# A hybrid decoder trunk on one core: high and low parts of transposed blocks split bank by bank

## The chip, the core and the metric
The kernel runs on one NeuronCore of a Trainium2 chip. Times are microseconds (us) of device time of one execution. TensorE (PE, with its weight loads as PEld) does the matmuls and transposes, VectorE (DVE) and ScalarE (ACT) read its results out of PSUM, GpSimd (POOL) does small arithmetic, and SyncE (SP) issues nearly all DMAs. PSUM has eight banks of 512 fp32 values per partition; this kernel keeps five for accumulators (`acc`) and three for transposes and small products (`pst`).

## What is computed
Two layers of a decoder on x of 256 x 1024 in fp32. Every sub-layer is normed before and after and added to x:

```python
for l in range(DEPTH):
    x = x + 0.5 * rmsnorm(swiglu(rmsnorm(x, ffn1_pre_g[l]), w_ffn1_in[l], w_ffn1_out[l]), ffn1_post_g[l])
    h = rmsnorm(x, mix_pre_g[l])
    (z, xbc, dt_raw, rq, rk, rv, rg, aq, ak, av, gate) = jnp.split(h @ w_in[l], offsets, axis=-1)
    ...
    branch = jnp.einsum('blmc,mcd->blmd', ys, w_branch[l])
    y = jnp.sum(gates * branch, axis=2) @ w_out[l]
    x = x + rmsnorm(y, mix_post_g[l])
    x = x + 0.5 * rmsnorm(swiglu(rmsnorm(x, ffn2_pre_g[l]), w_ffn2_in[l], w_ffn2_out[l]), ffn2_post_g[l])
```

`ys` stacks three mixers (a state-space one, retention, windowed attention). Inner width of the FFN is 2816.

## The kernel before, in words
The rows of x are two tiles of 128 tokens, t = 0 and 1. There are six phases: FFN 1, mixer, FFN 2 of layer 0, then the same of layer 1. Precision is kept by splitting every operand of a large matmul into a high part (rounded to fp32r) and a low part (what the rounding left), and by three matmuls for each block of 128 input channels (`mm3`, lines 86 to 89: high x low and high x high at line 88, low x high at line 89). ScalarE makes the high part with a copy, VectorE the low part with a subtraction that reads the source again (`split`, lines 66 to 69). Weights come in by DMA as `raw`, are split into `hl` (a ring of eight tiles, two blocks of channels each) and are used from there.

Activations must have channels on partitions, so they are transposed on TensorE, four blocks of 128 x 128 to a PSUM bank, and split on the way out. That happens in three places. `prenorm` (lines 169 to 190) transposes x of one t in two banks of four blocks; ScalarE writes each block's high part times the gain (line 182), VectorE its low part (line 185); the two squares of the row scale (line 150, in `sumsq`) are queued on ScalarE behind the last high part, and GpSimd turns their sums into the scale (lines 141 and 143). `transposed` (lines 153 to 164) does the same for the SwiGLU product `h` (two blocks to a bank, `hT`), for the mixers' outputs (`yT`, eight blocks) and their gated sum (`ysT`, four blocks), two blocks to one split. `att_kv` (lines 357 to 380) reads keys and values out of the accumulator: high parts `kh`, low parts `kl`, value `vn`, and multiplies them by a reversing matrix on TensorE (lines 375 and 379).

A phase begins inside the phase before it. `close` (line 308) runs its last four gemms and, within the last, calls the next prenorm for t = 0, whose transposes stand at a fixed place among the matmuls (lines 104 to 111). The next phase's first gemm uses that xT, unscaled: the row scale r is applied to the gemm's result. In the FFN the first result goes through silu (`sl`, line 125) and a product (`h`, line 127) to the transposes at line 161; the prenorm of t = 1 is called at the third step of the gemm of the second column chunk (lines 327 and 336). In the mixer the first result is that of `kvdt` (line 756): dt on VectorE (`dtx`, line 758), then `att_kv`; the prenorm of t = 1 is called in the middle of `aq0` (line 789). That prenorm needs x of t = 1, which `postnorm` (line 206) updates after the square and the product of lines 196 and 197.

The program order is a wish only. A scheduler with its own timeline puts the instructions of each engine in a fixed order, earlier program lines first among those that it holds to be ready. It also keeps two engines from using one PSUM bank at the same time, reads included, by waits in that order.

Of the kernel before, what the change touches and what calls it, by code (L numbers as in the profile page):

```python
# [8 lines left out]
F32 = mybir.dt.float32  # L9
R = mybir.dt.float32r  # L10
AF = mybir.ActivationFunctionType
ALU = mybir.AluOpType
AX = mybir.AxisListType

P = 128
# [25 lines left out]
class Trunk:  # L41
# [111 lines left out]
    def transposed(self, dst, src, t):  # L153
        nc = self.nc
        ts = slice(t * P, t * P + P)
        n = src.shape[-1] // P
        for q in range(0, n, 4):
            m = min(4, n - q)
            ps = self.pst.tile([P, 4, P], F32, tag="pst", name="pT")
            for j in range(m):  # L160
                nc.tensor.transpose(ps[:, j], src[:, (q + j) * P:(q + j + 1) * P], self.ident)  # L161
            for j in range(0, m, 2):
                d = dst[(q + j) // 2]
                self.split(d[:, :, 0, ts], d[:, :, 1, ts], ps[:, j:j + 2])

    def new_T(self, n, name):
        return [self.t4([2, 2, T], R, name) for _ in range(n)]
# [1 line left out]
    def prenorm(self, xT, t, g, r):  # L169

        nc = self.nc
        x = self.x
        ts = slice(t * P, t * P + P)
        made = []
        for q in range(0, KD, 4):
            ps = self.pst.tile([P, 4, P], F32, tag="pst", name="pT")
            for j in range(4):
                made.append(nc.tensor.transpose(ps[:, j], x[:, t, (q + j) * P:(q + j + 1) * P], self.ident))  # L178
            for j in range(4):
                k = q + j  # L180
                hi, lo = xT[k // 2][:, k % 2, 0, ts], xT[k // 2][:, k % 2, 1, ts]
                last = nc.scalar.activation(out=hi, in_=ps[:, j], func=AF.Copy, scale=g[:, k:k + 1])  # L182
                if k == 1:
                    self.opened = last
                nc.vector.scalar_tensor_tensor(out=lo, in0=ps[:, j], scalar=g[:, k:k + 1], in1=hi.bitcast(F32),  # L185
                                               op0=ALU.mult, op1=ALU.subtract)
        with self.tc.issue_after(last.ins):
            ss = self.sumsq([x[:, t, 0:512], x[:, t, 512:1024]], 1.0 / 32)
        self.rstd(ss, EPS, r)
        return made  # L190
# [166 lines left out]
    def att_kv(self, t, ps):  # L357
        nc, S = self.nc, self.S
        if t == 0:
            S["kT"] = self.t4([2, 2, T], R, "kT")  # L360
            S["av"] = self.t1([NT, P], name="av")
        k3 = ps[:, 0:P].rearrange("p (g d) -> p g d", g=2)
        kh = self.t1([2, 2, 64], R, name="kh")
        kl = self.t1([2, 2, 64], R, name="kl")
        r = S["r"][t]
        for o in range(2):
            nc.scalar.activation(out=kh[:, :, o], in_=k3, func=AF.Copy, scale=r)
            nc.vector.scalar_tensor_tensor(out=kl[:, :, o], in0=k3, scalar=r, in1=kh[:, :, o].bitcast(F32),
                                           op0=ALU.mult, op1=ALU.subtract)
        vn = self.t1([P], name="vn")  # L370
        nc.scalar.activation(out=vn, in_=ps[:, P:2 * P], func=AF.Copy, scale=r)
        pT = self.pbank()
        for g in range(2):
            for i, k in enumerate((kh, kl)):
                nc.tensor.matmul(pT[:, 2 * g + i], k[:, g].rearrange("p o d -> p (o d)"), self.revr,
                                 start=True, stop=True)
        self.copy(S["kT"][:, :, :, P - t * P:T - t * P], pT.rearrange("p (g o) n -> p g o n", g=2))
        pv = self.pbank()
        nc.tensor.matmul(pv[:, 0], self.revr.bitcast(F32), vn, start=True, stop=True)
        self.copy(S["av"][:, 1 - t], pv[:, 0])  # L380
# [587 lines left out]
```

## Time and profile before
| | |
|---|---|
| median of 3 runs | 1517.14 us (1514.94 to 1518.55) |
| the profiled execution | 1515.11 us |
| its span, first to last instruction | 1513.3 us |
| mean granted TensorE clock | 0.991 |
| instructions | 19964 |
| TensorE matmuls, waits of TensorE listed in the trace | 7277; 7 kinds, 18.3 us |

The profile shows one execution. Busy time is the share of the span in which an engine worked; for every idle stretch the trace names what ended it. The granted clock is that of TensorE, 1.00 being 2.4 GHz. Matmuls overlap, so the distance of their starts, not their length, is the pace.

### The profile page before, as it was taken

The page shows a single profiled execution, that of the slowest core. Times are in us where ns is not written, and L with a number is a line of the kernel's source. Part 1 is how long each engine was busy: PE and PEld are TensorE (multiplying, and loading weights), DVE is VectorE, ACT ScalarE, POOL GpSimd, SP SyncE. Part 2 cuts the span into 40 slices and gives each one's busy share as a digit, 9 for nine tenths or more (in the row PEclk, how much of TensorE's full clock was granted, in tenths as well). Part 3 has the DMA queues.
Part 4 walks back from the last instruction along what each step waited for, and adds up shares of the span by engine and source line. Part 5 has one row for each costly group of instructions (what it writes and reads, how often), then busy time and mean ns, then how long its engine had stood idle before and what let it go on. Part 6 is the DMA issues. An engine that isn't in the chain of part 4 may idle for free.

```text
span 1513.3 us, 19964 instructions
## 1 busy us (share of the span) xinstructions
PE 1488.2 (98%) x7277; PEld 1236.5 (82%) x7277; DVE 998.5 (66%) x1647; ACT 808.3 (53%) x1392; POOL 40.4 (3%) x80
## 2 busy tenths in 40 slices
PE   8999999999999999999999999999999999999998
PEld 6788878888888887888878888788888888778886
DVE  6654566778887676555566554767798876765643
ACT  6454465576554466444465454656665544655541
POOL 0000010000100000000000000000000000000000
PEclk9999999999999999999999999999999999999999
DMA  8654546545565555554555545564455655644551
GB/s 309 225 177 167 165 162 232 167 144 162 184 223 181 195 172 180 197 188 163 186 193 187 200 151 167 201 196 155 153 167 181 208 177 176 218 166 168 192 173 67
DMA packets 82771, 275.28 MB, mean 182 GB/s; under 512 B 11120, under 2 KB 15856, under 8 KB 82672
## 3 DMA queue, kind: packets, MB, share of 16 engines
q1 hardware_dynamic: 82384, 273.93, 53.9%
q8 instruction: 57, 0.93, 0.3%
q14 instruction: 42, 0.34, 0.1%
q10 hardware_dynamic: 288, 0.07, 0.0%
HBM read 272.86 MB, written 1.11 MB: 181 GB/s over the span
## 4 chain that ended last, share of the span: by engine, by line
PE 61%; issue 36%; DVE 1%; ACT 1%; POOL 1%; DMA 0%; SPq 0%; POOLq 0%; DVEq 0%; ACTq 0%
PE acc L88 32%; PE acc L89 16%; PE xbc L88 3%; PE xbc L89 2%; PE pT L161 1%; PE pS L420 1%; PE py L697 1%; PE po L455 1%; PE pT L178 1%; PE pb L447 1%; PE po L528 0%; DMA raw<-w_ffn_in 0%; DVE xT L185 0%; ACT xT L182 0%; ACT junk L150 0%
## 5 line engine op out<-in xcount | busy, mean ns | idle before, releaser
L88 PE MATMUL acc<-hl,xT 128*128 128x512 f32 (+1 forms) x2496 | 776.2, 393 | 3.1 <-DVE hl L69 3.0
L69 DVE TENSOR_TENSOR hl<-raw,hl 128x1024 fp32r<-128x1024 f32 (+2 forms) x544 | 592.2, 1105 | 183.0 <-ACT hl L68 164.0
L68 ACT CAST hl<-raw 128x1024 fp32r<-128x1024 f32 (+2 forms) x544 | 512.1, 956 | 255.4 <-PE acc L89 216.7
L88 PEld LDWEIGHTS acc<-hl,xT 128*128 128x128 f32 x2496 | 463.9, 189 | 95.6 <-DVE hl L69 3.2
L89 PE MATMUL acc<-hl,xT 128*128 128x512 f32 (+1 forms) x1248 | 486.7, 393 | 0.4 <-DVE xT L185 0.4
L89 PEld LDWEIGHTS acc<-hl,xT 128*128 128x128 f32 x1248 | 235.4, 189 | 49.0 <-DVE xT L185 1.4
L88 PE MATMUL acc<-hl,hT 128*128 128x512 f32 x704 | 216.9, 390 | 0.0
L88 PEld LDWEIGHTS acc<-hl,hT 128*128 128x128 f32 x704 | 131.7, 188 | 26.9
L89 PE MATMUL acc<-hl,hT 128*128 128x512 f32 x352 | 136.4, 389 | 0.0
L88 PE MATMUL acc<-hl,yT 128*128 128x512 f32 x384 | 122.1, 398 | 0.0
L127 DVE SCALAR_TENSOR_TENSOR h<-acc,pr,sl 128x256 f32<-128x256 f32 x88 | 42.2, 480 | 119.6 <-ACT sl L125 119.5
L125 ACT ACTIVATE sl<-acc,pr 128x256 f32<-128x256 f32 x88 | 41.9, 476 | 145.2 <-PE acc L89 144.8
L88 PEld LDWEIGHTS acc<-hl,yT 128*128 128x128 f32 x384 | 71.5, 188 | 16.7 <-issue 2.4
L89 PEld LDWEIGHTS acc<-hl,hT 128*128 128x128 f32 x352 | 66.1, 188 | 13.9
L89 PE MATMUL acc<-hl,yT 128*128 128x512 f32 x192 | 75.5, 393 | 0.0
L88 PE MATMUL xbc<-xT,hl 128*128 128x256 f32 x384 | 72.0, 286 | 0.0
L88 PEld LDWEIGHTS xbc<-xT,hl 128*128 128x128 f32 x384 | 60.2, 191 | 2.1 <-issue 1.5
L68 ACT CAST hT<-pT 128x256 fp32r<-128x256 f32 x88 | 32.6, 372 | 44.9 <-PE pT L161 44.8
L89 PE MATMUL xbc<-xT,hl 128*128 128x256 f32 x192 | 55.4, 289 | 0.0
L69 DVE TENSOR_TENSOR hT<-pT,hT 128x256 fp32r<-128x256 f32 x88 | 36.9, 420 | 26.9 <-ACT hT L68 26.9
L197 DVE TENSOR_TENSOR yg<-acc,gain 128x512 f32<-128x512 f32 x24 | 16.6, 690 | 46.9 <-ACT junk L196 46.9
L182 ACT ACTIVATE xT<-pT,pg 128x128 fp32r<-128x128 f32 x96 | 32.0, 364 | 21.7 <-DVE xT L185 13.9
(189 smaller groups left out, 1166.4 us busy)
## 6 DMA issues: line engine op xcount, KB each, us to landing
raw<-w_ffn_in SPq DMA_DIRECT2D x176, 512.0 KB, 4.8
raw<-w_main SPq DMA_DIRECT2D x152, 512.0 KB, 4.4
raw<-w_ffn_out SPq DMA_DIRECT2D x88, 512.0 KB, 4.7
raw<-w_branch SPq DMA_DIRECT2D x48, 512.0 KB, 4.4
raw<-w_out SPq DMA_DIRECT2D x16, 512.0 KB, 4.0
bias<-rows SPq DMA_DIRECT2D x8, 512.0 KB, 6.3
L<-acs SPq DMA_DIRECT2D x8, 512.0 KB, 6.2
gain<-b_gate SPq DMA_DIRECT2D x6, 512.0 KB, 5.1
```

The source lines that it names most:

```text
L68: nc.scalar.copy(out=hi, in_=src)
L69: nc.vector.tensor_tensor(out=lo, in0=src, in1=hi.bitcast(F32), op=ALU.subtract)
L88: return (mm(ps, xh, wl, start=start, stop=False), mm(ps, xh, wh, start=False, stop=False), mm(ps, xl, wh, start=False, stop=stop))
L89: mm(ps, xl, wh, start=False, stop=stop))
L125: self.last_silu = nc.scalar.activation(out=sl, in_=a, func=AF.Silu, scale=r)
L127: nc.vector.scalar_tensor_tensor(out=h, in0=b, scalar=r, in1=sl, op0=ALU.mult, op1=ALU.mult)
L161: nc.tensor.transpose(ps[:, j], src[:, (q + j) * P:(q + j + 1) * P], self.ident)
L178: made.append(nc.tensor.transpose(ps[:, j], x[:, t, (q + j) * P:(q + j + 1) * P], self.ident))
L182: last = nc.scalar.activation(out=hi, in_=ps[:, j], func=AF.Copy, scale=g[:, k:k + 1])
L197: self.nc.vector.tensor_tensor(out=y, in0=ps, in1=g[:, 512 * i:512 * i + 512], op=ALU.mult)
L420: nc.tensor.matmul(pS[:, i, :w], qT[t][:, hb + j + i], kT[:, g, hl, ks], start=hl == 0, stop=hl == 1)
L447: nc.tensor.transpose(pp[:, j], s[:, j, b * P:b * P + P], self.ident)
```

## The change
The number of instructions and their shapes stay. In `prenorm` all four high parts of a bank are issued before its four low parts. In `transposed` all high parts of a bank (one or two instructions) come before its low parts. In `att_kv` both high parts and the value come before both low parts.

```diff
@@ transposed
-            for j in range(0, m, 2):
-                d = dst[(q + j) // 2]
-                self.split(d[:, :, 0, ts], d[:, :, 1, ts], ps[:, j:j + 2])
+            parts = [(dst[(q + j) // 2], ps[:, j:j + 2]) for j in range(0, m, 2)]
+            for d, p in parts:
+                nc.scalar.copy(out=d[:, :, 0, ts], in_=p)
+            for d, p in parts:
+                nc.vector.tensor_tensor(out=d[:, :, 1, ts], in0=p, in1=d[:, :, 0, ts].bitcast(F32), op=ALU.subtract)
@@ prenorm
-            for j in range(4):
-                k = q + j
-                hi, lo = xT[k // 2][:, k % 2, 0, ts], xT[k // 2][:, k % 2, 1, ts]
+            part = lambda k, o: xT[k // 2][:, k % 2, o, ts]
+            for k in range(q, q + 4):
+                hi, j = part(k, 0), k - q
                 last = nc.scalar.activation(out=hi, in_=ps[:, j], func=AF.Copy, scale=g[:, k:k + 1])
                 if k == 1:
                     self.opened = last
-                nc.vector.scalar_tensor_tensor(out=lo, in0=ps[:, j], scalar=g[:, k:k + 1], in1=hi.bitcast(F32),
-                                               op0=ALU.mult, op1=ALU.subtract)
+            for k in range(q, q + 4):
+                nc.vector.scalar_tensor_tensor(out=part(k, 1), in0=ps[:, k - q], scalar=g[:, k:k + 1],
+                                               in1=part(k, 0).bitcast(F32), op0=ALU.mult, op1=ALU.subtract)
@@ att_kv
         for o in range(2):
             nc.scalar.activation(out=kh[:, :, o], in_=k3, func=AF.Copy, scale=r)
+        vn = self.t1([P], name="vn")
+        nc.scalar.activation(out=vn, in_=ps[:, P:2 * P], func=AF.Copy, scale=r)
+        for o in range(2):
             nc.vector.scalar_tensor_tensor(out=kl[:, :, o], in0=k3, scalar=r, in1=kh[:, :, o].bitcast(F32),
                                            op0=ALU.mult, op1=ALU.subtract)
-        vn = self.t1([P], name="vn")
-        nc.scalar.activation(out=vn, in_=ps[:, P:2 * P], func=AF.Copy, scale=r)
```

## Rows read from the trace of the kernel before
**Rows 1.** The page, part 1: busy time of each engine, share, instructions.
```profile
PE 1488.2 (98%) x7277; PEld 1236.5 (82%) x7277; DVE 998.5 (66%) x1647; ACT 808.3 (53%) x1392; POOL 40.4 (3%) x80
```
**Rows 2.** Waits of TensorE: waiting engine and line, for what: us, times, longest.
```profile
PE pT L161 <- DVE h L127: 6.4, 3, 2.4
PE pb L375 <- ACT kh L367: 4.9, 2, 2.5
PE acc L88 <- DVE hl L69: 3.0, 1, 3.0
PE pb L375 <- DVE kl L368: 1.7, 2, 0.9
```
**Rows 3.** Waits of all engines, ScalarE's for the low part in prenorm.
```profile
ACT xT L182 <- DVE xT L185: 13.9, 35, 0.8
```
**Rows 4.** Timeline, mixer of layer 0: start, busy us, engine, line [idle before, releaser].
```profile
197.44 0.36 ACT L182 ACTIVATE xT<-pT,pg 128x128 fp32r<-128x128 f32 x1
...
198.74 1.05 ACT L68 CAST hl<-raw 128x1024 fp32r<-128x1024 f32 x1 [0.94 <-PE acc L89]
...
202.75 0.63 ACT L182 ACTIVATE xT<-pT,pg 128x128 fp32r<-128x128 f32 x2 [0.78 <-DVE xT L185]
...
203.15 0.61 DVE L185 SCALAR_TENSOR_TENSOR xT<-pT,pg,xT 128x128 fp32r<-128x128 f32 x2 [0.18 <-ACT xT L182]
...
203.80 0.37 ACT L182 ACTIVATE xT<-pT,pg 128x128 fp32r<-128x128 f32 x1 [0.42 <-DVE xT L185]
...
204.59 0.37 ACT L182 ACTIVATE xT<-pT,pg 128x128 fp32r<-128x128 f32 x1 [0.42 <-DVE xT L185]
...
206.80 0.56 POOL L143 TENSOR_TENSOR pr<-v,mhalf 128x1 f32<-128x1 f32 x1
```
**Rows 5.** Timeline of TensorE, same stretch: before the wait, and back at full pace.
```profile
206.40 0.29 PE L89 MATMUL acc<-hl,xT 128*128 128x272 f32 x1
...
214.11 0.62 PE L88 MATMUL acc<-hl,xT 128*128 128x512 f32 x2
```
**Rows 6.** Chain that ended last, in order of time: start, us, what, how many.
```profile
22.97 1.36 PE acc L88 x6
...
562.03 0.87 PE pT L178 x8
```
**Rows 7.** Busy time by stretch: PE, PEld, DVE, ACT, POOL, granted clock, DMA share, GB/s.
```profile
211.00:212.00 1.00, 1.00 (x7) 1.00 (x7) 0.20 (x1) 0.58 (x1) 0.00 (x0) 0.50 0.01 4
```
**Rows 8.** Timeline, second FFN of layer 0.
```profile
572.76 0.39 PE L89 MATMUL acc<-hl,xT 128*128 128x512 f32 x1
...
573.23 1.28 ACT L125 ACT_TABLE_LOAD   x1
...
574.52 0.47 ACT L125 ACTIVATE sl<-acc,pr 128x256 f32<-128x256 f32 x1
...
575.57 0.69 PE L161 MATMUL pT<-identr,h 128*128 128x128 f32 x2 [2.42 <-DVE h L127]
...
579.07 0.62 PE L88 MATMUL acc<-hl,xT 128*128 128x512 f32 x2
```
**Rows 9.** Timeline, layer 1: first FFN, mixer, second FFN.
```profile
763.94 0.39 PE L89 MATMUL acc<-hl,xT 128*128 128x512 f32 x1
...
764.84 0.47 ACT L125 ACTIVATE sl<-acc,pr 128x256 f32<-128x256 f32 x1 [0.36 <-POOL pr L143]
...
770.48 0.62 PE L88 MATMUL acc<-hl,xT 128*128 128x512 f32 x2
...
954.61 0.29 PE L89 MATMUL acc<-hl,xT 128*128 128x272 f32 x1
...
964.95 0.87 PE L88 MATMUL acc<-hl,xT 128*128 128x272 f32 x4
...
1322.20 0.39 PE L89 MATMUL acc<-hl,xT 128*128 128x512 f32 x1
...
1329.78 0.63 PE L88 MATMUL acc<-hl,xT 128*128 128x512 f32 x2
```

## The prediction
> **What bounds the kernel now.** I read the page's first part, then TensorE's own waits, then the engines in order of time around them. TensorE is busy 98% of the span, VectorE 66%, ScalarE 53% [rows 1]: only time in which TensorE stands still or runs slowly can be saved. Its largest waits in mid-run are few: three for the SwiGLU product `h`, 6.4 us together, two for the key's high part `kh`, 2.45 each, and right behind them two for `kl`, 0.86 each; the one for weights (`hl`) is at the very start [rows 2]. These seven stand where a phase begins: both mixers, the second FFN of both layers, the first FFN of layer 1.
>
> In front of each runs a prenorm. In the first mixer ScalarE makes a high part, waits 0.42 us for VectorE's low part, makes the next: a step of 0.79 us per block (203.80 to 204.59), although two high parts that need not wait for each other take 0.63 together, two low parts 0.61 [rows 4]. ScalarE waited so 35 times, 13.9 us in all [rows 3]. High and low part write different places, so it is the shared PSUM bank that puts them in turn. The first of eight high parts starts at 197.44, the last at 204.59; only behind it come the two squares for the row scale and GpSimd's power, done at 207.36 [rows 4], and only then `dtx` and `kh`, for which TensorE waits.
>
> A phase start costs more than the wait. After it the granted clock falls to 0.50, the lower of the two levels, 1.2 of 2.4 GHz [rows 7], until TensorE has worked on for some time. So I count from the last matmul before the wait to the first one back at full pace, less the work between. Six 512-wide matmuls take 1.36, one 0.227; eight transposes take 0.87, one 0.11 [rows 6]; a 272-wide matmul I put at 0.13 (estimate: 0.227 by its columns, rounded up).
> - Mixer, layer 0: 206.53 to 214.11 [rows 5], 7.6; six small matmuls 0.65, eight transposes 0.87, three matmuls 0.68: 2.2. Lost 5.4, of it 2.45 + 0.86 = 3.3 waiting.
> - Mixer, layer 1: 954.74 to 964.95 [rows 9], 10.2; the same with nine matmuls: 3.6. Lost 6.6.
> - Second FFN, layer 0: 572.99 to 579.07 [rows 8], 6.1; two transposes of `h` 0.22, eight 0.87, three matmuls 0.68: 1.8. Lost 4.3.
> - Second FFN, layer 1: 1322.43 to 1329.78 [rows 9], 7.35; with six matmuls 2.45. Lost 4.9.
> - First FFN, layer 1: 764.17 to 770.48 [rows 9], 6.3; 2.45. Lost 3.9.
>
> Together 25.1 us, 1.7% of the span: the pool.
>
> **The change, part by part.** No instruction is added or removed and none changes its size; SP's and GpSimd's queues keep their entries, and no DMA moves. What changes is the order on ScalarE and VectorE and so the number of turns per bank, four before, one after.
>
> *Prenorm.* After the change eight high parts follow each other: 0.37 + 7 x 0.26 (the second of the pair of 0.63) = 2.2 us, instead of 197.44 to 204.96, 7.5 us, in which two weight casts of 1.05 also ran [rows 4]. I take it that the scheduler keeps the eight together, because the prenorm stands earlier in the program than the weights that it now lets past; if it doesn't, see the second case. ScalarE is then done at about 199.7, 5.3 us earlier, and squares, power and scale with it: the scale at about 202.1 instead of 207.4.
>
> *Mixers.* TensorE's work before `kh` is the kv gemm and the first five steps of `aq0`; it ran them interleaved, as xT came in pieces, until 206.5 [rows 5]. These are 24 x 0.13 = 3.1 and 15 x 0.227 = 3.4 us, so they begin near 200.0. With xT whole by then the kv gemm ends at 203.1. Behind it `dtx` (put at one low part, 0.35), two high parts, `vn` and two low parts: 0.35 + 0.37 + 2 x 0.26 + 0.61 and hops, some 2 us, to 205.1. The 15 matmuls cover that with 1.4 to spare. So the whole loss goes: 5.4 + 6.6 = 12.0. In `att_kv` itself the first low part now waits for all three ScalarE reads: 0.26 + 0.26 later; behind it on VectorE stand the two `x` updates, and for those the next transposes wait. Cost 0 under that cover, 0.5 a layer without it.
>
> *First FFN, layer 1.* `sl` waited for the row scale [rows 9], itself behind the squares. With the scale about 5 us early and the first gemm no longer interleaved with six matmuls of the next (1.36), silu and product, 1.05 from 574.52 to 575.57 [rows 8], are covered. 3.9 goes.
>
> *Second FFNs.* Here the chain starts at the end of the gemm, not at the scale: a table load of 1.28, silu, product; 572.99 to 575.57 [rows 8], 2.6. It cannot shrink; the change only puts the six matmuls, 1.36, over it. 1.2 remains, or 0.35 if the eight transposes of `x` also go ahead of `h`. Whether the clock still falls after such a gap no row shows; the nearest is the first FFN, whose wait of 1.6 (6.4 less 2 x 2.4 [rows 2]) left 3.9 - 1.6 of other loss behind, so I leave its cost in. Recovered 1.2 + 1.2 = 2.4; with the clock held it would be 6.8, with the gap unchanged 0. The Trainium skill (ScalarE: Activation LUTs, "What ACT_TABLE_LOAD costs") gives a switch of tables about 2.66 us, as a drain follows the load; by it 1.4 more would stay open in each of the two, and this term would be 0. The trace disagrees: `sl` starts 0.01 behind the load [rows 8].
>
> *Start of the run.* The first prenorm runs while the first weights are still landing. The low part of block 0 comes three high parts, 0.8, later than now, the last ones earlier. Between +0.8 and -0.8; I take 0.
>
> *Prenorms of the second half* (t = 1) run beside matmuls of t = 0: 0. *`yT` and `ysT`*: no wait of TensorE names them, gate and branch gemms run meanwhile; 0, and 0.8 a turn, one step of rows 4, if that cover were gone. `hT` has one pair to a bank and does not change.
>
> Sum: 12.0 + 3.9 + 2.4 = 18.3 us. The profiled execution took 1515.1, 1.8 over its span; that gives 1496.8. The median of the runs, 1517.1, is 2.0 above it: **1499**. Bounds of this case: 1493 (the clock term of the second FFNs too, and some at the start) to 1506 (a third less).
>
> **Rivals.**
> *Half of it.* The scheduler fixes each engine's order by its own clock, and now it slots weight casts between high parts (198.74 [rows 4]). If it goes on doing so, three casts of 1.05 to a prenorm, the scale comes 2.2 us earlier, not 5.3. In the mixers 3.3 of waiting becomes 1.1 and the fallen clock stays: 4.4. The first FFN still gets its 3.9, the second ones 0.7 each: 9.7, **1507**. For it: casts stand there now. Against: they do because a high part was not ready.
>
> *The wait only moves.* TensorE's order is fixed too. If the scheduler puts the `kh` matmuls or the transposes of `h` right behind the gemm, without the filling work, TensorE waits through the whole chain: 2 us in the mixers, 2.6 in the second FFNs, 1.0 in the first. With the clock that is nearly today's loss: 3 saved, **1514**, which is no change. For it: the chain now stands at the end of all filling work. Against: other work is ready then.
>
> *Slower.* Eight high parts, 2.2, and the squares, some 1.9 (204.96 to the power at 206.80 [rows 4]), now hold ScalarE in one piece for 4.1 us, and the weight casts of the phase queue behind it, VectorE's low casts after them. In the mixer the cast at 198.74 would start at 201.6, and the next at 202.6. If such a cast is due when the block begins, TensorE waits up to 4.1 + 1.05 for it, plus 2.0 of clock as in the mixer (5.4 less 3.3 of waiting): at each of five phase starts, less the 18.3 saved, at most +17; with half the block exposed, 2.6 + 2.0 each, +5: **1522**. It decides once a cast ends later than its matmul is due. Against: TensorE never waits for `hl` in mid-run [rows 2], so casts have slack of an unknown size.
>
> **Numbers.** Forecast 0.52, half 0.26, moved 0.13, slower 0.09. Faster by over 0.2% (3.0 us, about what a measurement of this kernel can tell from no change) is the first two, 0.78; within it 0.13; slower 0.09. The range takes in the first two with their bounds: 1491 to 1512.
>
> **What would show it.** Right: in each prenorm four high parts in one run of about 1.15 us and four low ones behind; the row scale some 5 us earlier; no TensorE wait for `kh` or in the first FFN; clock 1.00 through both mixers' starts; about 1 us of wait for `h` left in the second FFNs. Half: casts between the high parts. Moved: `kh` right behind the last kv matmul, with a wait. Slower: TensorE waits for `hl`. I am wrong if the waits go and the span does not follow, or if it falls while they stay.

## The result and the profile after

The changed kernel took 1500.13 us, the median of four executions (1497.97 to 1500.52); the kernel before, beside it, 1516.04 (1513.78 to 1518.55). The ratio is 0.9893, with a 95% interval of 0.988 to 0.9905: about 16 us saved, as forecast within 1.1 us. The profiled execution took 1497.97 against 1515.11 before, 17.1 less; its span is 1496.2.

Page of the changed kernel, part 1 (busy time, share, instructions):

```profile
PE 1476.6 (99%) x7277; PEld 1228.2 (82%) x7277; DVE 996.1 (67%) x1647; ACT 798.4 (53%) x1392; POOL 43.2 (3%) x80
```

Against [rows 1] the counts of instructions are the same; TensorE is busy for 11.6 us less with the same matmuls: they ran at full pace for more of the time. Waits of TensorE in the changed kernel (waiting engine and line, for what: us, times, longest):

```profile
PE pT L161 <- DVE h L127: 6.0, 3, 2.4
PE acc L88 <- DVE hl L69: 2.9, 1, 2.9
PE pb L379 <- ACT kh L370: 2.8, 2, 1.4
```

Against [rows 2]: the two waits for `kl` are gone, those for `kh` fell from 2.45 to 1.38 each, those for `h` hardly moved, and `hl` still delays TensorE at the start alone. ScalarE's 35 waits for the low part [rows 3] are gone from the list.

Timeline of the changed kernel, mixer of layer 0, to be read beside [rows 4] (start, busy us, engine, line [idle before, releaser]):

```profile
196.42 2.17 ACT L184 ACTIVATE xT<-pT,pg 128x128 fp32r<-128x128 f32 x8
...
197.69 2.15 DVE L188 SCALAR_TENSOR_TENSOR xT<-pT,pg,xT 128x128 fp32r<-128x128 f32 x8
...
198.43 0.68 ACT L150 ACTIVATE junk<-x 128x512 bf16<-128x512 f32 x1
...
199.05 2.04 ACT L68 CAST hl<-raw 128x1024 fp32r<-128x1024 f32 x2
...
200.94 0.68 ACT L150 ACTIVATE junk<-x 128x512 bf16<-128x512 f32 x1
...
202.79 0.56 POOL L143 TENSOR_TENSOR pr<-v,mhalf 128x1 f32<-128x1 f32 x1
...
204.58 1.42 DVE L209 SCALAR_TENSOR_TENSOR x<-yg,r,x 128x512 f32<-128x512 f32 x2 [1.43 <-POOL r L143]
...
205.91 0.23 DVE L762 SCALAR_TENSOR_TENSOR dtx<-acc,pr,dtb 128x16 f32<-128x16 f32 x1
...
206.23 0.63 ACT L370 ACTIVATE kh<-acc,pr 128x128 fp32r<-128x128 f32 x2 [3.81 <-DVE dtx L762]
...
206.91 0.33 PE L379 MATMUL pb<-revr,kh 128*128 128x128 f32 x1 [1.38 <-ACT kh L370]
```

Eight high parts run in one piece of 2.17 us (2.2 forecast, 7.5 before), the low parts behind them in 2.15. The casts no longer stand among the high parts: two of them stand between the two squares instead, so that the scale is done at 203.35 and not at 202.1. What holds up `kh` now is new: VectorE waits 1.43 us for GpSimd's closing scale of the phase before, does two updates of x, and only then `dtx`. Before, `dtx` came first (207.68) and the updates at 208.60, behind the first `kl` (lines with `e3_attkv` below).

Timeline of the changed kernel, second FFN of layer 0, to be read beside [rows 8]:

```profile
568.10 1.28 ACT L125 ACT_TABLE_LOAD   x1 [3.14 <-PE acc L89]
569.40 0.47 ACT L125 ACTIVATE sl<-acc,pr 128x256 f32<-128x256 f32 x1
569.91 0.49 DVE L127 SCALAR_TENSOR_TENSOR h<-acc,pr,sl 128x256 f32<-128x256 f32 x1 [2.45 <-ACT sl L125]
...
570.45 0.44 PE L161 MATMUL pT<-identr,h 128*128 128x128 f32 x2 [2.42 <-DVE h L127]
...
570.72 1.04 PE L180 MATMUL pT<-identr,x 128*128 128x128 f32 x8
...
572.30 0.62 PE L88 MATMUL acc<-hl,xT 128*128 128x512 f32 x2
```

The wait is the same 2.42, because TensorE's order still runs the six matmuls of the next gemm among those of the first. But the transposes now run at full pace. Busy time by stretch in the changed kernel (PE, PEld, DVE, ACT, POOL, granted clock, DMA share, GB/s):

```profile
568.00:575.00 7.00, 4.58 (x26) 3.96 (x26) 3.07 (x10) 5.64 (x15) 0.00 (x1) 1.00 0.24 98
```

Before, the granted clock fell behind each of the five phase starts; in this execution of the changed kernel it stays at 1.00 behind all five. In the first FFN of layer 1 `sl` no longer waits for a scale [rows 9], and the wait for `h` is shorter:

```profile
757.67 0.47 ACT L125 ACTIVATE sl<-acc,pr 128x256 f32<-128x256 f32 x1 [3.25 <-PE acc L89]
...
758.71 0.44 PE L161 MATMUL pT<-identr,h 128*128 128x128 f32 x2 [1.15 <-DVE h L127]
```

By the prediction's own count (last matmul before the wait to the first at full pace, less the work between) the changed kernel loses 1.8 us in the mixer of layer 0 (205.37 to 209.38 less 2.2), 1.8 in that of layer 1 (945.34 to 950.70 less 3.56), 2.7 in each second FFN (567.86 to 572.30 less 1.77; 1307.78 to 1312.91 less 2.45) and 1.4 in the first FFN (757.41 to 761.25 less 2.45). Recovered are 3.6, 4.8, 1.6, 2.2 and 2.5: 14.7 of the pool of 25.1. Between these two executions the start of the run differs by another 1.1: the eight transposes of t = 1 began at 13.98 in the changed kernel, at 15.10 before; whether the change did that is taken up with `e10_again` below. Some 1.3 of the 17.1 is spread over the run and not traced.

### The profile page after: what moved, and what is told of

It is laid out like the page before. It is cut to its first block, busy times and chain, and to the rows that moved or that the text cites. A ratio compares the mean times of both kernels' runs of the same rounds, so it can differ in the third digit from the quotient of the medians.

```text
span 1496.2 us, 20006 instructions
## 1 busy us (share of the span) xinstructions
PE 1476.6 (99%) x7277; PEld 1228.2 (82%) x7277; DVE 996.1 (67%) x1647; ACT 798.4 (53%) x1392; POOL 43.2 (3%) x80
## 4 chain that ended last, share of the span: by engine, by line
PE 72%; issue 24%; DMA 2%; ACT 1%; POOL 1%; DVE 0%; POOLq 0%; DVEq 0%; ACTq 0%
PE acc L88 39%; PE acc L89 20%; PE xbc L88 3%; PE xbc L89 2%; PE pT L161 1%; PE pS L424 1%; PE py L701 1%; PE po L459 1%; PE pb L451 1%; DMA x<-x 1%; PE po L532 0%; DMA cw<-w_conv 0%; PE pT L180 0%; ACT xT L184 0%; DMA gain<-ffn_post_g 0%
## 5 line engine op out<-in xcount | busy, mean ns | idle before, releaser
L439 ACT ACTIVATE s<-s,nm 128x128 f32<-128x128 f32 (+1 forms) x64 | 28.4, 445 | 34.7 <-DVE nm L433 34.6
```

Of the source, the lines that this page charges most:

```text
L439: nc.scalar.activation(out=s[:, j], in_=s[:, j], func=AF.Exp, bias=nm[:, j:j + 1], accum_out=l[:, j:j + 1])
```

## Experiments

Each is timed beside the kernel before on the same chip. The medians of before were 1516.67 (first four), 1517.37 (next four) and 1516.97 (last four).

### One part of the change at a time

`e1_prenorm` is the kernel before with the prenorm's reordering alone, `e2_transposed` with that of `transposed` alone, `e3_attkv` with that of `att_kv` alone; each is that part of the diff above and nothing else.

> Only the prenorm's part of the change. My theory (the blocks' turns in the prenorm set the row scale, and five phase starts wait for it): all of the gain, 1500 +- 2 us, with the waits of TensorE for kh near 1.4 us each or a little over, as in the changed kernel. Rival (a part of the gain comes from the transposed mixer outputs, from the key split, or from a reshuffle elsewhere): 1504 to 1512.

> Only the mixer outputs' and their sum's part (yT, ysT). My theory: no wait of TensorE hangs on them, so 1516 +- 3 us, and the seven waits at the five phase starts stand as before. Rival (they carry a part): under 1512.

> Only the key split's part. My theory: the row scale comes as late as before, so TensorE still waits about 2.4 us for kh in each mixer; the second wait, for kl (0.86 each before), may go: 1514 to 1517 us. Rival (the key split closes the mixers' waits, 12 us of loss, by itself): 1504 to 1508.

| | median (range) | ratio, 95% interval | waits of TensorE: `h`, `kh`, `kl` |
|---|---|---|---|
| e1_prenorm | 1505.82 (1505.35 to 1507.84) | 0.9938 [0.9917, 0.9959] | 6.0, 3.8, none |
| e2_transposed | 1516.18 (1512.25 to 1517.75) | 0.9997 [0.9982, 1.0011] | as before |
| e3_attkv | 1513.33 (1510.63 to 1515.03) | 0.9976 [0.9963, 0.9989] | 6.4, 3.8, 0.5 |

The prenorm carries most of the change, 10.9 us of it; the expectation had given it all, and its rival, a part elsewhere, came true. `transposed` is worth nothing that can be measured, as the prediction had it. The key split is worth 3.3 us, a little more than its expectation (1514 to 1517), and the prediction had put it at nothing. Its splits were on the path. Timeline of the kernel before, mixer of layer 0:

```profile
207.68 0.23 DVE L758 SCALAR_TENSOR_TENSOR dtx<-acc,pr,dtb 128x16 f32<-128x16 f32 x1
...
208.34 0.35 DVE L368 SCALAR_TENSOR_TENSOR kl<-acc,pr,kh 128x128 fp32r<-128x128 f32 x1 [0.43 <-ACT kh L367]
208.60 1.41 DVE L206 SCALAR_TENSOR_TENSOR x<-yg,r,x 128x512 f32<-128x512 f32 x2
208.72 0.37 ACT L367 ACTIVATE kh<-acc,pr 128x128 fp32r<-128x128 f32 x1 [0.42 <-DVE kl L368]
...
210.31 0.37 ACT L371 ACTIVATE vn<-acc,pr 128x128 f32<-128x128 f32 x1 [1.22 <-DVE kl L368]
```

The second `kh` waits for the first `kl`, the value for the second. In `e3_attkv` the two `kh` follow each other, and its profile shows 2.3 us less of waiting for `kh` and `kl` than [rows 2]. The three parts sum to 14.7 us, and the whole change gave 15.9.

The prenorm alone leaves waits only 1.0 us longer than the whole change does, but is 5.7 us slower. Most of the rest shows in the clock: in its profiled execution the granted clock fell in the mixer of layer 1 (0.91 over 940 to 960) and in both second FFNs, behind waits of 1.90, 2.42 and 2.42. In the mixer of layer 0, behind a wait of 1.92, it did not.

### Two turns per bank instead of one

```diff
-            for k in range(q, q + 4):
-                hi, j = part(k, 0), k - q
-                last = nc.scalar.activation(out=hi, in_=ps[:, j], func=AF.Copy, scale=g[:, k:k + 1])
...
+            for k0 in (q, q + 2):
+                for k in (k0, k0 + 1):
+                    last = nc.scalar.activation(out=part(k, 0), in_=ps[:, k - q], func=AF.Copy, scale=g[:, k:k + 1])
...
+                for k in (k0, k0 + 1):
+                    nc.vector.scalar_tensor_tensor(out=part(k, 1), in0=ps[:, k - q], scalar=g[:, k:k + 1],
+                                                   in1=part(k, 0).bitcast(F32), op0=ALU.mult, op1=ALU.subtract)
```

> The changed kernel, but the prenorm splits a bank in two turns (two high parts, two low, two high, two low) instead of one; before there were four. My theory (the number of turns sets when the scale comes): in between, the scale of the first mixer about half way between 207.4 and 203.4 us of the span, and 1504 to 1511 us. Rival (what counts is only that high parts no longer alternate one by one): as the changed kernel, 1500 +- 2. Other rival (any second turn lets the weight casts in again): as before, 1514 or more.

It took 1504.97 us (1502.31 to 1507.71), ratio 0.9927 [0.9898, 0.9956], an interval that just touches that of the whole change. TensorE waits 4.4 us for `kh` (2.8 in the changed kernel) and 6.0 for `h`. The scale of the first mixer is done at 203.79, only 0.4 later than with one turn (0.8 by the start of its own prenorm, which stood 0.4 earlier), not half way as expected: the casts stand among the high parts again, but both squares follow at once. So two turns instead of one keep most of the earlier scale. `kh` waits longer all the same: in this order all 15 matmuls of `aq0` run before the last ones of the kv gemm, and none is left over the chain. Span against span the kernel is 7.4 us longer than with one turn; 1.6 of that are the waits for `kh`, and most of the rest goes with the clock, which fell at three starts.

### What is left: the waits for `h` and `kh`

These four start from the changed kernel.

`e5_x_behind_h`: in the second FFNs the update of x for t = 1 is put behind `h` on VectorE, so that the transposes of x no longer follow at once.

```diff
-        nc.vector.scalar_tensor_tensor(out=h, in0=b, scalar=r, in1=sl, op0=ALU.mult, op1=ALU.mult)
+        self.behind = nc.vector.scalar_tensor_tensor(out=h, in0=b, scalar=r, in1=sl, op0=ALU.mult, op1=ALU.mult)
...
+            if behind is not None:
+                self.after(u, behind)
...
+        def second():
+            if defer:
+                self.postnorm(1, [yg[1, 0], yg[1, 1]], ss[1], 4 * EPS, False, self.behind)
+            return nxt(1)
```

> The changed kernel, but in the second FFNs VectorE updates x of t = 1 behind the product h instead of ahead of it, so that the eight transposes of x come some microseconds behind those of h, as in the kernel before. Changed kernel: 1500.1 us, ratio 0.989, wait for h 2.42 each, clock 1.00 behind it. Theory (what follows the wait at once decides on the clock): same waits for h, one more short wait for x, clock below 1.0 at 560 to 580 and at 1300 to 1320; some 2 us a layer, 1504, ratio 0.992. Rival (the clock has nothing to do with it): clock 1.00, waits for x of about 1 us each at most, 1501 to 1502, ratio 0.990.

1503.72 us (1502.01 to 1505.35), ratio 0.9912 [0.9897, 0.9927]. Waits: `h` 6.0, `kh` 2.8, x 0.7 in three. The clock fell behind the second FFN of layer 0 and stayed at 1.00 behind that of layer 1, with the same edit and the same wait of 2.42 in both. So neither theory holds as put: what follows the wait does not decide alone. The time is 3.6 us above the changed kernel's first median and 2.3 above its second (`e10_again` below), and the intervals touch.

`e6_silu_early`: a silu of one column, right behind the last square of the phase before, loads the table under the gemm.

```diff
-        self.nc.scalar.activation(out=j, in_=ps, func=AF.Square, scale=scale / 32, accum_out=ss[:, i:i + 1])
+        self.sq = self.nc.scalar.activation(out=j, in_=ps, func=AF.Square, scale=scale / 32, accum_out=ss[:, i:i + 1])
...
+        if i == 2:
+            self.after(nc.scalar.activation(out=self.small(1, "w"), in_=self.mhalf, func=AF.Silu), self.sq)
```

> The changed kernel with one silu of a single column more on ScalarE behind the two squares of each second FFN's prenorm, so that the table load of 1.28 us runs under the first gemm. Theory (the chain table load, silu, product behind the gemm is the whole wait): wait for h 2.42 becomes 1.15, as in the first FFN of layer 1, whose chain has no load; 1.27 less in each of two layers, 1497.5, ratio 0.9875. Rival (the load only moves: it holds up the silu from the other side, or squares or casts behind it pay): wait stays above 2, 1500, ratio 0.989.

1496.44 us (1495.46 to 1496.85), ratio 0.9863 [0.9848, 0.9878]. Timelines of this kernel, ScalarE and then TensorE:

```profile
566.15 1.28 ACT L329 ACT_TABLE_LOAD   x1
...
569.30 0.48 ACT L125 ACTIVATE sl<-acc,pr 128x256 f32<-128x256 f32 x1 [1.65 <-PE acc L89]
```

```profile
570.35 0.44 PE L161 MATMUL pT<-identr,h 128*128 128x128 f32 x2 [1.15 <-DVE h L127]
```

The load ran under the gemm, and the wait became 1.15 in both layers, as the theory had it. The median fell by 3.7 us, 1.1 more than the two waits; the clock stayed at 1.00 behind all five starts. Span against span it is 1.4 us (1496.2 to 1494.8), as this execution stood 1.2 us later than that of the changed kernel when the first mixer's prenorm began (196.45 against 195.27).

`e7_h_behind_x`: TensorE's order gets the cover that the prediction had counted on; the first transposes of `h` come behind the eight of x.

```diff
+            late = where == (1, 0)
+            def both():
+                made = self.second()
+                if late:
+                    for tr in self.transposed(hT[0:1], held, 0):
+                        self.after(tr, made[-1])
+                return made
...
+            if late and (c, t) == (0, 0):
+                held = h
+            else:
+                self.transposed(hT[c:c + 1], h, t)
```

> The changed kernel with the first two transposes of h put behind the eight transposes of x of t = 1 on TensorE, in the second FFNs and in the first FFN of layer 1. This is the cover that the prediction counted on (0.35 left of the wait). Theory (the wait is there because TensorE's order has no work over the chain): with eight transposes, 0.87, and the split behind them ahead, waits for h fall from 6.0 to some 3.5 or less, 1497.5 to 1499, ratio 0.988. Rival (x is not ready then, or its transposes are needed no earlier): a wait for x takes its place, 1500 or more, ratio 0.989 to 0.991.

1491.17 us (1490.94 to 1492.09), ratio 0.9831 [0.9814, 0.9847]: 9.0 us below the changed kernel, more than either theory gave. Waits of TensorE:

```profile
PE acc L88 <- DVE hl L69: 2.9, 2, 2.1
PE pb L393 <- ACT kh L384: 2.8, 2, 1.4
PE acc L256 <- DVE warm L253: 1.4, 1, 1.4
PE pT L162 <- DVE h L127: 0.2, 1, 0.2
```

And its timeline in the second FFN of layer 0:

```profile
567.66 1.03 PE L182 MATMUL pT<-identr,x 128*128 128x128 f32 x8
567.90 1.28 ACT L125 ACT_TABLE_LOAD   x1 [3.15 <-PE acc L89]
...
568.45 0.71 PE L88 MATMUL acc<-hl,xT 128*128 128x512 f32 x2
```

The transposes of x and the next matmuls run over table load, silu and product, and the three waits for `h`, 6.0 us, go to 0.2. Span against span the gain is 6.7 us (1496.2 to 1489.5), which is the three losses of 2.7, 2.7 and 1.4 counted above; the medians differ by more because the changed kernel's profiled execution was its fastest (below).

`e8_dtx_first`: VectorE does `dtx` ahead of the two updates of x.

```diff
+            if behind is not None:
+                self.after(u, behind)
...
+                self.postnorm(1, [yg[1, 0], yg[1, 1]], ss[1], 4 * EPS, False, self.behind)
...
-            nc.vector.scalar_tensor_tensor(out=dtx[:, t], in0=ps[:, 256:272], scalar=r[t], in1=self.dtb,
+            self.behind = nc.vector.scalar_tensor_tensor(out=dtx[:, t], in0=ps[:, 256:272], scalar=r[t], in1=self.dtb,
```

> The changed kernel with VectorE's order changed at the mixers' starts: dtx first, then the two x updates of t = 1, which in the changed kernel stand ahead of dtx and wait 1.43 us for their own scale. Theory (these two hold up dtx, and dtx holds up kh): the wait for kh, 1.38 in each layer, goes or falls under 0.4, a wait for x of up to 0.5 may come; 2 us less, 1498, ratio 0.988. Rival (kh waits for the end of the kv gemm itself, x only stood in a gap): wait for kh stays over 1.0, 1500, ratio 0.989.

1498.83 us (1497.32 to 1499.51), ratio 0.9879 [0.9864, 0.9893]. Its timeline in the mixer of layer 0:

```profile
204.60 0.23 DVE L772 SCALAR_TENSOR_TENSOR dtx<-acc,pr,dtb 128x16 f32<-128x16 f32 x1 [1.11 <-PE acc L89]
...
204.87 0.63 ACT L380 ACTIVATE kh<-acc,pr 128x128 fp32r<-128x128 f32 x2 [2.10 <-DVE dtx L772]
204.91 1.41 DVE L209 SCALAR_TENSOR_TENSOR x<-yg,r,x 128x512 f32<-128x512 f32 x2
...
205.71 0.22 PE L389 MATMUL pb<-revr,kh 128*128 128x128 f32 x1
```

`kh` comes 1.4 us earlier and TensorE no longer waits for it; 0.3 us for `kl` are left. So the two updates of x were what held up `kh`; the six matmuls behind the kv gemm, as many as in the changed kernel, now cover the chain. The median is 1.3 us lower, not clear of the noise (the intervals overlap), and the span did not follow, 1496.9 against 1496.2: in this execution the clock fell behind both second FFNs, which this kernel leaves as they were. Its timeline and its clock there, to be read beside those of the changed kernel above:

```profile
569.36 0.69 PE L161 MATMUL pT<-identr,h 128*128 128x128 f32 x2 [2.42 <-DVE h L127]
...
572.75 0.63 PE L88 MATMUL acc<-hl,xT 128*128 128x512 f32 x2
```

```profile
568.00:575.00 7.00, 5.64 (x23) 5.00 (x24) 3.07 (x10) 4.66 (x15) 0.34 (x2) 0.76 0.14 55
```

Same order, same wait; from the transposes of `h` to the third group of gemm matmuls it took 3.39 us (569.36 to 572.75) where the changed kernel took 1.85 (570.45 to 572.30). The fall cost 1.5 us here.

### All three, and the clock from execution to execution

`e9_all` has the last three edits together. `e10_again` is the changed kernel as it is, once more. `e11_shift8` and `e12_shift18` repeat transposes of `h` in the first FFN (8 and 18 of them), so that all that follows stands later in the run:

```diff
-    def transposed(self, dst, src, t):
+    def transposed(self, dst, src, t, rep=1):
...
-            for j in range(m):
+            for j in list(range(m)) * rep:
...
-            self.transposed(hT[c:c + 1], h, t)
+            self.transposed(hT[c:c + 1], h, t, 5 if where == (0, 0) and c == 5 and t == 0 else 1)
```

> The changed kernel with all three edits of the last runs: the silu table loaded under the first gemm, the first transposes of h behind those of x, dtx ahead of the two x updates. Measured alone: 1496.4, 1491.2, 1498.8 against 1500.1 for the changed kernel. Theory (each closes a gap of its own, and the early table is worth nothing where the gap is covered): no wait for h over 0.3, wait for kh gone, kl 0.3 left; 1491.2 less the 2.5 us of the two waits for kh: 1488.7, between 1487 and 1490, ratio 0.981. Rival (what closes one gap opens another, or the clock falls elsewhere, as behind dtx put first): 1491 to 1495, ratio 0.983 to 0.986.

> The changed kernel as it is, once more, for the same run of the chip. If the clock behind its gaps of 2.42 us is a matter of chance from execution to execution: times spread over 4 to 6 us between 1497 and 1508, with one or two falls of the clock in the profile. If it belongs to the program: 1498 to 1501 in every run, ratio 0.989, clock 1.00 in mid-run.

> The changed kernel with eight repeated transposes of h (0.9 us of work) in the first FFN of layer 0, so that all later stages stand 0.9 us later in the run; no engine's order around the five phase starts is changed. If the clock depends on the gap and the work around it alone: clock 1.00 in mid-run as in the changed kernel, 1501.0. If it also depends on where in the run the gap stands: it falls in one to three of the phase starts, some 2 us each, 1503 to 1507, with the waits as they were (h 6.0, kh 2.8).

> The same with eighteen repeated transposes (2.0 us), a second place in the run. Gap alone: 1502.1, clock 1.00. Place in the run: waits unchanged, falls at one to three phase starts, not the same ones as with eight; 1504 to 1508.

| | median (range) | ratio, 95% interval | second FFN, layer 0 and 1: clock |
|---|---|---|---|
| e9_all | 1489.99 (1489.04 to 1490.75) | 0.9822 [0.9808, 0.9837] | held, held |
| e10_again | 1501.43 (1497.90 to 1503.07) | 0.9895 [0.988, 0.991] | held, fell |
| e11_shift8 | 1502.20 (1501.17 to 1502.89) | 0.9903 [0.9888, 0.9917] | fell, held |
| e12_shift18 | 1501.90 (1501.62 to 1503.87) | 0.9906 [0.9889, 0.9922] | held, fell |

`e9_all` is the best: 27 us below the kernel before and 10 to 11 below the changed one (1500.13, and 1501.43 in `e10_again`). Its waits of TensorE:

```profile
PE acc L88 <- DVE hl L69: 2.6, 1, 2.6
PE acc L258 <- DVE warm L255: 1.4, 1, 1.4
PE pT L162 <- DVE h L127: 0.4, 1, 0.4
PE pb L405 <- DVE kl L400: 0.4, 2, 0.2
```

Nothing over 0.4 is left in mid-run, against 0.3 expected. The median lies 1.3 above the sum of 1488.7, just inside the range that was given, 1487 to 1490.

`e10_again` bears on the clock. It is the same program, and its four executions took 1497.90, 1501.13, 1501.74 and 1503.07 us, at mean clocks of 0.998, 0.998, 0.996 and 0.994. In the profiled one of them, 1501.13, the clock fell in the second FFN of layer 1; timeline and clock of `e10_again` there:

```profile
1311.26 0.69 PE L161 MATMUL pT<-identr,h 128*128 128x128 f32 x2 [2.42 <-DVE h L127]
...
1314.72 0.61 PE L88 MATMUL acc<-hl,xT 128*128 128x512 f32 x2
```

```profile
1312.00:1314.00 2.00, 2.00 (x10) 1.90 (x9) 0.42 (x1) 1.52 (x6) 0.00 (x0) 0.50 0.00 0
```

The same stage of the changed kernel in its profiled execution:

```profile
1310.36 0.44 PE L161 MATMUL pT<-identr,h 128*128 128x128 f32 x2 [2.42 <-DVE h L127]
...
1312.21 0.62 PE L88 MATMUL acc<-hl,xT 128*128 128x512 f32 x2
```

3.46 us against 1.85: the same program and the same wait, and the clock falls in one execution and holds in another, for 1.6 us. The spans of these two executions differ by more, 3.1 us. Another 1.0 lies at the start of the run. The changed kernel there:

```profile
12.61 0.62 PE L88 MATMUL acc<-hl,xT 128*128 128x512 f32 x2
...
13.98 1.03 PE L180 MATMUL pT<-identr,x 128*128 128x128 f32 x8
```

And `e10_again`:

```profile
13.08 1.05 PE L88 MATMUL acc<-hl,xT 128*128 128x512 f32 x2
...
14.99 1.03 PE L180 MATMUL pT<-identr,x 128*128 128x128 f32 x8
```

In one execution two matmuls pass in 0.46 us from 12.61 on, in the other they still take 0.86 at 13.08, half the pace, and the transposes of t = 1 come at 14.99 instead of 13.98. Before the change they came at 15.10, so of the 1.1 us counted for the start above, 0.1 is left in this execution of the same program. Over all profiles they begin between 13.28 and 15.93 with the reordered prenorm (eleven executions) and between 15.10 and 15.99 with the old (three). That the change shortens the start is therefore not shown.

The two shifted kernels, with the waits at the phase starts as they were, show one fall each, in different layers, and lie 0.8 and 0.5 us above `e10_again`, no more than their added work of 0.9 and 2.0 us. The times came near those expected with the clock held (1501.0 and 1502.1), the falls were those of the other case. Of the place in the run deciding, nothing more is seen than the unshifted program shows from one execution to the next.

The Trainium skill (TensorE: Matmul & The Clock Gate, "What's actually happening") says that the window in which the chip judges TensorE's activity runs freely and is not started by the kernel; falls by chance between executions of one program agree with that, though no run here shows the mechanism.

Over all fourteen profiled executions the phase starts read so: none of 25 waits of 1.14 to 1.40 us was followed by a lower clock, all three of 1.52 to 1.56 were, four of the six waits for `kh` of 1.90 to 2.19 were (in `e1`, `e3`, `e4`), all four of 2.44 and 2.45 with a second one for `kl` behind them were (before, `e2`), and of the 22 waits for `h` of 2.42 to 2.44 in the second FFNs 16 were. Six of those 22 belong to the kernels with the old prenorm (before, `e2`, `e3`), and all six fell; of the other 16 ten did. What makes the difference between the six and the sixteen was not settled.

## Why the prediction was right, step by step

**The path.** Right. The turns per bank were what made the prenorm long, the row scale late and so TensorE idle at the phase starts. `e1_prenorm` shows that this part carries the gain, and the eight high parts took the 2.2 us worked out for them.

**The scale at 202.1.** It came at 203.35, later by 1.2: the step "ScalarE is then done at about 199.7, and squares, power and scale with it" overlooked that the casts, pushed out from among the high parts, could be slotted between the squares (199.05 to 201.09). Measured against the run's own course, which stood 1 us earlier there, the scale gained some 3 us and not 5.3; the 2.04 of the two casts are nearly all of the difference.

**Mixers: 12.0 forecast, 8.4 measured.** Two sub-steps failed. Of "the 15 matmuls cover that" only six stood behind the kv gemm; the prediction had put the interleaving down to xT coming "in pieces", but TensorE's order interleaves the other nine with the gemm though xT is whole from 199.84 on (197.69 and 2.15). And the chain was longer than "`dtx`, two high parts ...": VectorE's order had the two updates of x ahead of `dtx`, waiting for a scale of their own. The prediction had placed those updates behind the low parts and given them no price. `e8_dtx_first` shows that they were the rest of the wait, and that with `dtx` first even the six matmuls are enough. That the clock cost would go with the wait was right: none of the waits of 1.36 to 1.40 for `kh` was followed by a fall.

**`att_kv`: 0 forecast, 3.3 measured alone.** The prediction looked at what the reordering could cost under cover, and not at what it gave: `e3_attkv` took away 2.3 us of waits for `kh` and `kl` even with the prenorm unchanged. In the whole change this is part of the 8.4 above and does not come on top.

**First FFN: 3.9 forecast, 2.5 measured.** `sl` no longer waits for the scale, as said, and the clock holds. But 1.15 of waiting stays, as the six matmuls remain interleaved and cover nothing.

**Second FFNs: 2.4 forecast, 3.8 measured in the profiled execution, for another reason.** The step "the change only puts the six matmuls over it" failed: the wait stayed 2.42, which the bound "0 with the gap unchanged" had allowed for. The gain came from the clock, which the prediction had left in, and from transposes of x that were ready at once. `e10_again` shows that this part is not certain: with a fall, 1.6 of it goes again. In the changed kernel, its repeat and the two shifted ones three of eight such waits were followed by a fall; at 1.55 us the two layers would then lose 2 x 3/8 x 1.55 = 1.2 us on average (an estimate from eight waits). The start of the run, 1.0 us apart in the two profiles of one program, adds to that; together they are of the size of the 2.2 us by which the changed kernel's median lies above its fastest execution.

**Table load.** After the change too `sl` starts 0.02 us behind the load's end (568.10 + 1.28 = 569.38, and 569.40), and the early load of `e6_silu_early` took 1.27 off the wait, the load alone. What ScalarE did ahead of the load, in the kernel before:

```profile
572.95 0.20 ACT L196 ACTIVATION_READ_ACCUMULATOR junk<-acc 128x1 f32 x1
```

It ends at 573.15, and the load starts at 573.23 [rows 8]. The Trainium skill (ScalarE: Activation LUTs, "What ACT_TABLE_LOAD costs") counts a drain of 1.38 us with each switch of tables; the trace disagrees, as neither the 0.08 us ahead of this load nor the 0.01 us behind it has room for one.

**Start of the run.** 0 forecast, with bounds of 0.8 to either side; 1.1 between the two profiled executions, 0.1 against `e10_again`. With that spread the runs neither confirm nor refute the forecast of nothing.

**The sum.** 18.3 forecast, 17.1 in the profiled execution, 15.9 between medians. Too much for the mixers (3.6) and the first FFN (1.4), too little for the second FFNs (1.4); the start (1.1) and what was not traced (1.3) were put at nothing. The phase starts together gave 14.7 of the 18.3, and errors on both sides made the total better than its terms: that 1499 came within 1.1 us of 1500.13 is in part luck.

**Its own signs.** The runs of high parts (2.17 for eight) and the clock through both mixers' starts came as described. The scale came 3 us earlier and not some 5, waits of 1.38 for `kh` and of 1.15 in the first FFN were left where none should be, and 2.42 for `h` in the second FFNs where about 1 should be. That the span "falls while they stay" was named as a sign of being wrong, and in the second FFNs that happened: 3.8 us went with the waits unchanged.

**The rivals.** Casts no longer stood between the high parts, but two between the squares: a small piece of *half of it* came true. *The wait only moves* describes the FFNs: `h` stands right behind the gemm without filling work, and `e7_h_behind_x` shows what the filling would have been worth. In the mixers 1.38 of 2.45 stayed in each, with the six matmuls as filling. It was wrong in expecting the clock's cost to stay. *Slower* did not come: no wait for `hl` in mid-run.

## What to carry to other kernels

Where two engines read one PSUM bank and the trace shows them taking turns, issue one engine's reads of the bank together: here the gain showed where the end of that block is what a phase start waits for, and was nothing elsewhere (`transposed`). Then read each engine's fixed order at the new critical point: here two updates ahead of a small `dtx`, and two transposes placed ahead of eight that were ready, were worth another 10 us. Close or shorten a TensorE gap even where its own length is small, as a fall of the granted clock behind it cost some 1.5 us more here, and time such a kernel several times, as one execution can have the clock and the next not.

## What was not expected of the hardware

That the same program, with the same wait of 2.42 us, loses the full clock behind it in one execution and keeps it in another, as told above. No wait of 1.40 us or less at a phase start was followed by a lower clock in these profiles. The times of the kernels without such waits spread over 1.1 us (`e7_h_behind_x`), 1.4 (`e6_silu_early`) and 1.7 (`e9_all`), those of the changed kernel over 2.6 and 5.2; but `e11_shift8`, which has both waits of 2.42, spread over 1.7 too, so that steadier times are not shown with four executions each.
